# Decoder step: main-stream turns half as long, attention streams reordered, two r tiles moved from plain units to a Strassen pair

## The chip, the cores and the metric

The kernel runs on one core of one Trainium2 chip. The metric is device time in microseconds for one launch; a smaller number is better. The time given is the median of several runs; the profile is of one further execution.

## The reference

One step of a one-layer hybrid decoder, all in float32. Prompt: 512 rows; samples: 8 x 4 = 32 rows; width 2048. The kernel keeps both in one activation of 544 columns.

```python
z = rmsnorm(x, g_pre) @ w_in            # 15 parts: q,k,v, index q/k/w, gates, bu,bv, cq, ra,rb,rc
# A: index scores pick k keys per query, then softmax attention over them (8 heads, 4 kv heads)
I  = einsum(relu(qi . ki), wi);  idx = top_k(I, 128 prompt / 256 sample of 2052)
oa = softmax(q k[idx]^T / sqrt(128)) v[idx]
# B: chunked mixing
ob = bu * (tril(w_s) @ rmsnorm(bv) + b_s)
# C: 4-head attention into 256 memory tokens
oc = softmax(rmsnorm(cq) mk^T / 16) mv
m  = sum over n in a,b,c of sigmoid(r_n) * ((o_n * silu(g_n)) @ w_p_n)
y  = x + m @ w_out
```

The outputs are y for prompt and samples, and the new k, v, index k, memory k and v, and the normalized bv of the samples. The prompt attends over its own 512 keys; the samples gather keys and values from a paged cache.

## The kernel before

Every large product is done in float32r with both factors split in a high and a low part, three products each (`wh x_h`, `wh x_l`, `wl x_h`). ScalarE makes the high part of a weight tile, VectorE or POOL the low part. The moving operand has 544 columns and is done in two halves of 272.

A *unit* (`columns`, L600) is one tile of 128 output columns: 16 k-tiles, three products, two halves. A *pair* (class `Pair`, L503) is two such tiles done by Strassen's scheme: seven products of half size in place of eight.

The work is staged, and each stage ends when all its streams have ended:
- memory keys and values and the transposed activations;
- the middle stage, "in": 41 units for qi, ki, cq, then k, v, q, then bv, followed by `NI` = 43 of the 48 r tiles (r tiles go through a sigmoid and out to DRAM, `r_done`, L823);
- "turn": `NT` = 3 more r units while the operands for Strassen's scheme are formed on VectorE;
- "fast": 17 pairs: bu and bg, cg, ag, and last what is left of the r tiles, 48 - 43 - 3 = 2, one pair;
- merge, and the output projection.

Each engine works through its instructions in the order in which the program issues them, and this order is made by `Flow.run` (L206) when the program is built. Main stream and side streams are Python generators. `Flow` keeps an estimated clock for every engine. In each round every side stream whose due time has been reached gets up to six steps, then the main stream gets one step, up to its next `yield`. In `columns` that is every second k-tile, so twelve products. `yield due(t)` waits until the estimate says that tile t is ready; `yield have("x")` until flag x is set; `yield idle(a)` until VectorE's estimated clock is no more than a us ahead of TensorE's.

The side streams of the middle stage, in their order:
- `post_stream`: the job of every finished z tile: rope, norms, transposes, stores (`job_k`, `job_q`, `job_bv`; flags `kvq0` to `kvq3`, `bv`);
- `att_stream` (L1742): the index scores of samples and prompt, four memory heads (`mem_attend`, L1591), the mixing of branch B (which waits for `bv`), four prompt heads (`attend`, L1527);
- `prompt_choice`: the prompt's top-k on VectorE, throttled by `idle`;
- `sample_stream`: `sample_choice` (32 rounds of max, index, replace on VectorE), `sample_work`: gather keys, dot products on VectorE, softmax, gather values on POOL's queue, products `ps<-v` on TensorE;
- `cross_stream`: the samples' attention into the memory cache, mostly dot products on VectorE, throttled.

PSUM for side work: two banks `pa`, one `pp`, one `ps`. `post_stream` uses `pp`, the attention `pa`, the sample and cross streams `ps`. A softmax row block is `softmax_rows`: scale and maximum on VectorE, exponential on ScalarE, reciprocal and product on VectorE.

Of the kernel before, what the change touches and what calls it, by code (L numbers as in the profile page):

```python
# [34 lines left out]
NW3 = 2  # L35
NZ = 3
PI = 0.5
NI, NT = 43, 3
NG = 5
NX, CA, CD, MA, MB = 3, 4, 6, 4, 0  # L40
SLACK = 0.4
# [193 lines left out]
def decoder_step(  # L235
# [364 lines left out]
    def columns(w, c0, m, kts, rhs, done, cond=None, ready=None, over=None):  # L600

        n = PW // 128
        parts = [(w[h * n * 128:(h + 1) * n * 128, c0:c0 + m].rearrange("(k p) c -> p k c", p=128), n, m)
                 for h in range(kts // n)]

        def emit(z, h, hl):
            for kk in range(n):
                kt = h * n + kk
                if ready and not ready(kt)():
                    yield ready(kt)  # L610
                xh, xl = rhs(kt)
                if ready:
                    yield due(xl)
                for wt, xt in ((0, 0), (0, 1), (1, 0)):
                    for a in range(2):
                        PE.matmul(z[:m, a, :TH], hl[wt][:, kk, :], (xh, xl)[xt][:, a * TH:(a + 1) * TH],
                                  start=(kt == 0 and wt + xt == 0), stop=(kt == kts - 1 and wt == 1))
                if over:
                    over()
                if kk % 2 == 1:  # L620
                    yield

        return Unit(parts, emit, lambda z: done(z[:, :, :TH]), cond)

# [440 lines left out]
    def rope_rows(src, blk, cos, sin, p):  # L1065

        sw = TP_("sw")
        for b in range(p // blk):
            o, i = b * blk, (b ^ 1) * blk
            S.copy(sw[o:o + blk], src[i:i + blk])  # L1070
        V.tensor_mul(src[:p], src[:p], cos[:p])
        G.tensor_mul(sw[:p], sw[:p], sin[:p])
        yield due(sw)
        V.tensor_add(src[:p], src[:p], sw[:p])

# [66 lines left out]
    def norm_rope(zc, tb):  # L1142

        tp = yield from prompt_tr(zc)
        y = v4(TP_("y"))
        S.copy(y, tp)
        ss = sm([128, 4], "ss4", bufs=2)
        for t in range(4):
            S.activation(junk_a, y[:, t, :], AF.Square, accum_out=ss[:, t:t + 1])
        yield due(ss)  # L1150
        r = rsqrt(ss, 128, 128, 4)
        for t in range(4):
            V.tensor_scalar(y[:, t, :], y[:, t, :], r[:, t:t + 1], None, op0=OP.mult)
        o, u = v4(TP_("yo")), v4(TP_("yu"))
        V.tensor_mul(o[:, :, :64], y[:, :, :64], tb[:, 0])
        V.tensor_mul(u[:, :, :64], y[:, :, 64:], tb[:, 1])
        G.tensor_mul(u[:, :, 64:], y[:, :, :64], tb[:, 3])
        V.tensor_mul(o[:, :, 64:], y[:, :, 64:], tb[:, 2])
        V.tensor_sub(o[:, :, :64], o[:, :, :64], u[:, :, :64])
        yield due(u)  # L1160
        V.tensor_add(o[:, :, 64:], o[:, :, 64:], u[:, :, 64:])
        yield due(o)
        return o
# [361 lines left out]
        V.tensor_scalar(p_ap, p_ap, ri, None, op0=OP.mult)  # L1525

    def attend(g):  # L1527
        yield have("kvq%d" % g, "sel1", "sel2", "sel3")
        raws = []
        for d, c in ((k_d, g), (q_d, 2 * g), (q_d, 2 * g + 1), (v_d, g)):  # L1530
            raw = v4(PT("araw"))
            SP.dma_start(raw, rows4(d)[:, :, c * 128:(c + 1) * 128])
            raws.append(raw)
        parts = []
        for raw in raws:
            yield due(raw)
            if raw is not raws[3]:
                tp = yield from psum("pa")
                for t in range(4):
                    tr(tp[:, t * 128:(t + 1) * 128], raw[:, t, :])  # L1540
                yield due(tp)
                raw = v4(tp)
            hl = KK(), KK()
            split_from(v4(hl[0]), v4(hl[1]), raw)
            parts.append(hl)
        kk, qq, vv = parts[0], parts[1:3], parts[3]
        yield due(vv[1])
        for blk in range(4):
            nk = (blk + 1) * 128
            cols = slice(blk * 128, (blk + 1) * 128)  # L1550
            ss = []
            for r in range(2):
                s = yield from psum("pa")
                mm3(s[:, :nk], [x[:, cols] for x in qq[r]], [x[:, :nk] for x in kk])
                ss.append(s)
            pts = []
            for r in range(2):
                yield due(ss[r])
                pt = PT()
                mx = sm([128, 1], "mx")  # L1560
                V.tensor_tensor_reduce(pt[:, :nk], ss[r][:, :nk], selb[blk], 1.0, TAKEN, OP.add, OP.max, mx)
                softmax_rows(pt[:, :nk], mx, SA)
                pts.append(pt)
            yield due(*pts)
            pT = {}
            for k0 in range(0, blk + 1, 2):
                n = min(2, blk + 1 - k0)
                tp = yield from psum("pa")
                for kb in range(n):
                    for r in range(2):  # L1570
                        tr(tp[:, kb * 256 + r * 128:kb * 256 + (r + 1) * 128],
                           pts[r][:, (k0 + kb) * 128:(k0 + kb + 1) * 128])
                yield due(tp)
                ph, pl = PH(), PH()
                split_from(ph[:, :n * 256], pl[:, :n * 256], tp[:, :n * 256])
                for kb in range(n):
                    pT[k0 + kb] = [x[:, kb * 256:(kb + 1) * 256] for x in (ph, pl)]
            yield due(pl)
            o = yield from psum("pa")
            for kb in range(blk + 1):  # L1580
                mm3(o[:, :256], [x[:, kb * 128:(kb + 1) * 128] for x in vv], pT[kb],
                    start=kb == 0, stop=kb == blk)
            yield due(o)
            ot = OT()
            S.copy(ot, o[:, :256])
            yield due(ot)
            SP.dma_start(oa_d.rearrange("(h d) t -> d h t", d=128)[:, 2 * g:2 * g + 2, cols],
                         ot.rearrange("p (r q) -> p r q", r=2))
        flags["att%d" % g] = 1

    def mem_attend(h):  # L1591
# [27 lines left out]
        mk = KK(), KK()  # L1619
        split_from(mk[0], mk[1], tp)  # L1620
        yield due(mk[1], cq[1][1])
        for b2 in range(2):
            s = yield from psum("pa")
            for bb in range(2):
                blk = b2 * 2 + bb
                for dt in range(2):
                    mm3(s[:, bb * 256:(bb + 1) * 256], [x[:, blk * 128:(blk + 1) * 128] for x in cq[dt]],
                        [x[:, dt * 256:(dt + 1) * 256] for x in mk], start=dt == 0, stop=dt == 1)
            yield due(s)
            pt = PT()  # L1630
            S.copy(pt, s)
            mx = sm([128, 2], "mx2", bufs=2)
            V.tensor_reduce(mx, pt.rearrange("p (b m) -> p b m", b=2), axis=AX.X, op=OP.max)
            for bb in range(2):
                softmax_rows(pt[:, bb * 256:(bb + 1) * 256], mx[:, bb:bb + 1],
                             cms[:, h, b2 * 2 + bb:b2 * 2 + bb + 1])
            yield due(pt)
            tp = yield from psum("pa")
            for mt in range(2):
                for bb in range(2):  # L1640
                    tr(tp[:, mt * 256 + bb * 128:mt * 256 + (bb + 1) * 128],
                       pt[:, bb * 256 + mt * 128:bb * 256 + (mt + 1) * 128])
            yield due(tp)
            ph, pl = PH(), PH()
            split_from(ph, pl, tp)
            yield due(pl)
            o = yield from psum("pa")
            for dt in range(2):
                for mt in range(2):
                    mm3(o[:, dt * 256:(dt + 1) * 256],  # L1650
                        [x[:, mt * 256 + dt * 128:mt * 256 + (dt + 1) * 128] for x in mv],
                        [x[:, mt * 256:(mt + 1) * 256] for x in (ph, pl)], start=mt == 0, stop=mt == 1)
            yield due(o)
            ots = OT(), OT()
            for dt in range(2):
                S.copy(ots[dt], o[:, dt * 256:(dt + 1) * 256])
            yield due(*ots)
            for dt in range(2):
                SP.dma_start(oc_d[(2 * h + dt) * 128:(2 * h + dt + 1) * 128, b2 * 256:(b2 + 1) * 256], ots[dt])
# [82 lines left out]
    def att_stream():  # L1742
        yield from sample_index()
        yield from prompt_index()
        for h in range(4):
            yield from mem_attend(h)
        yield from mixing()
# [660 lines left out]
```

## Time and profile before

| | |
|---|---|
| median of 3 runs | 2300.39 us (2296.32 to 2301.41) |
| the profiled execution, time | 2297.85 us |
| its span, first to last instruction | 2296.1 us |
| granted TensorE clock, mean | 0.992 |
| PE / PEld busy | 2223.4 / 2138.6 us |
| DVE / ACT / POOL busy | 1686.7 / 964.5 / 283.8 us |

PE is TensorE's products, PEld its weight loads, DVE VectorE, ACT ScalarE, POOL GpSimd, SP the queue that issues most DMAs. Products are pipelined, so the mean duration of one (some 290 ns) is longer than the distance from one to the next, and a busy PE is not a PE at its peak. Names such as `z<-x,whi` are the tiles written and read: `z` the accumulator of a unit, `zs` that of a pair, `pa`, `pp` and `ps` the side banks. The whole kernel issues through one helper, so all rows have line L61; tiles tell the operations apart.

### The profile page before, as it was taken

To read this page: it belongs to the slowest core of one execution; us is meant where nothing else is said; L and a number is where in the kernel's file an instruction comes from. 1 tells how busy PE (TensorE), PEld (TensorE's weight loads), DVE (VectorE), ACT (ScalarE), POOL (GpSimd) and SP (SyncE) were. 2 spreads that over 40 slices of the span, in tenths; PEclk is the share of its full clock that TensorE was granted. 3 is DMA by queue.
4 is the path that set the end of the run, shared out by engine and by line. 5 is a ranking of instruction groups with operands and counts; after the bars stand their busy time and mean duration, and the time that the engine had idled before them with its cause. 6 is when DMAs were issued, how large, how long until landed. Compare 5 with 4: busy or idle time off the path is not lost. (4 is left out here: it accounts for less than half of the span.)

```text
span 2296.1 us, 46130 instructions
## 1 busy us (share of the span) xinstructions
PE 2223.4 (97%) x17057; PEld 2138.6 (93%) x17057; DVE 1686.7 (73%) x4658; ACT 964.5 (42%) x1944; POOL 283.8 (12%) x275
## 2 busy tenths in 40 slices
PE   8899999899999999999999998999999999999999
PEld 6699999899999998999999985999999999999999
DVE  7843557999889899666889514998899635567786
ACT  6544454454454432444544322444444422233443
POOL 1121220010010011001333343000000001200000
PEclk9999999999999999999999999999999999999999
DMA  7654434556556766446788776344454645444453
GB/s 245 220 173 109 124 101 112 167 147 190 164 170 197 221 196 189 137 122 180 251 272 272 221 214 173 100 127 134 128 163 143 204 135 172 143 132 136 128 158 88
DMA packets 497535, 382.17 MB, mean 166 GB/s; under 512 B 35786, under 2 KB 427068, under 8 KB 497308
## 3 DMA queue, kind: packets, MB, share of 16 engines
q1 hardware_dynamic: 485532, 341.45, 50.7%
q0 software_dynamic: 11776, 37.76, 5.0%
q8 instruction: 134, 2.20, 0.4%
q14 instruction: 93, 0.76, 0.1%
HBM read 329.81 MB, written 49.30 MB: 165 GB/s over the span
## 5 line engine op out<-in xcount | busy, mean ns | idle before, releaser
L61 PE MATMUL z<-x,whi 128*128 128x272 f32 (+1 forms) x5696 | 960.9, 291 | 0.0
L61 PEld LDWEIGHTS z<-x,whi 128*128 128x128 f32 (+1 forms) x5696 | 805.9, 188 | 19.3 <-issue 12.6
L61 DVE TENSOR_TENSOR wlo<-raw,whi 128x512 fp32r<-128x512 f32 (+1 forms) x613 | 427.0, 706 | 274.7 <-ACT whi L61 264.8
L61 ACT CAST whi<-raw 128x512 fp32r<-128x512 f32 (+1 forms) x660 | 402.8, 619 | 537.8 <-PE z L61 349.3
L61 PE MATMUL z<-x,wlo 128*128 128x272 f32 (+1 forms) x2848 | 589.8, 289 | 0.9 <-DVE wlo L61 0.9
L61 PEld LDWEIGHTS z<-x,wlo 128*128 128x128 f32 (+1 forms) x2848 | 445.5, 189 | 1.3 <-DVE wlo L61 1.3
L61 PE MATMUL zs<-x,whi 128*128 128x272 f32 x1536 | 293.5, 289 | 2.2 <-ACT whi L61 1.4
L61 PEld LDWEIGHTS zs<-x,whi 128*128 128x128 f32 x1536 | 242.6, 189 | 2.7 <-ACT whi L61 1.7
L61 PE MATMUL zs<-x,wlo 128*128 128x272 f32 x768 | 223.0, 290 | 1.3 <-DVE wlo L61 1.3
L61 ACT CAST whi<-wsum 128x512 fp32r<-128x512 f32 x192 | 119.2, 622 | 131.7 <-PE zs L61 97.3
L61 PE MATMUL zs<-oh,wlo 128*128 128x272 f32 x576 | 167.0, 290 | 1.7 <-DVE wlo L61 1.7
L61 PE MATMUL zs<-oh,whi 128*128 128x272 f32 x576 | 167.0, 290 | 0.2 <-ACT oh L61 0.2
L61 PE MATMUL zs<-ol,whi 128*128 128x272 f32 x576 | 165.6, 288 | 0.4 <-DVE ol L61 0.4
L61 PE MATMUL z<-oh,whi 128*128 128x272 f32 x768 | 159.2, 289 | 3.7 <-DVE zc L61 2.6
L61 PE MATMUL z<-ol,whi 128*128 128x272 f32 x768 | 158.8, 288 | 0.4 <-DVE ol L61 0.2
L61 PE MATMUL z<-oh,wlo 128*128 128x272 f32 x768 | 158.4, 287 | 0.0
L61 PEld LDWEIGHTS zs<-x,wlo 128*128 128x128 f32 x768 | 145.0, 189 | 1.5 <-DVE wlo L61 1.5
L61 DVE TENSOR_TENSOR wlo<-wsum,whi 128x512 fp32r<-128x512 f32 x181 | 121.5, 683 | 13.8 <-ACT whi L61 13.8
L61 POOL TENSOR_TENSOR wlo<-raw,whi 128x512 fp32r<-128x512 f32 x47 | 63.5, 1352 | 526.8 <-ACT whi L61 431.3
L61 PEld LDWEIGHTS z<-oh,whi 128*128 128x128 f32 x768 | 120.4, 188 | 4.1 <-issue 2.8
L61 PEld LDWEIGHTS z<-ol,whi 128*128 128x128 f32 x768 | 120.7, 189 | 0.8 <-DVE ol L61 0.8
L61 PEld LDWEIGHTS z<-oh,wlo 128*128 128x128 f32 x768 | 120.2, 188 | 0.0
(340 smaller groups left out, 3119.7 us busy)
## 6 DMA issues: line engine op xcount, KB each, us to landing
raw<-in_w_in_dram SPq DMA_DIRECT2D x480, 256.0 KB, 3.2
raw<-in_w_mem_kv_dram SPq DMA_DIRECT2D x64, 256.0 KB, 4.9
qbc<-cqs_d SPq DMA_DIRECT2D x64, 256.0 KB, 5.0
qbc<-qs_d SPq DMA_DIRECT2D x32, 512.0 KB, 5.6
raw<-in_w_out_dram SPq DMA_DIRECT2D x64, 256.0 KB, 2.7
kc<-in_cache_mem_k_dram SPq DMA_DIRECT2D x32, 256.0 KB, 4.5
raw<-in_w_pb_dram SPq DMA_DIRECT2D x32, 256.0 KB, 2.6
raw<-in_w_pc_dram SPq DMA_DIRECT2D x32, 256.0 KB, 2.7
```

The lines of the kernel that those rows point to most:

```text
L61: r = f(*args, **kwargs)
```

## The change

The constant `NI` goes from 43 to 41, so two r tiles more are left for pairs: the fast stage has 18 pairs. The main stream yields after every k-tile. Two kinds of multiplication go from POOL to VectorE. `att_stream` waits for all k, v, q and bv tiles before the memory heads. In `attend` the scores of a block are issued ahead of the transposes of the block before; transposes and outputs go to bank `pp`. In `mem_attend` both score groups are issued first, then both softmaxes, then transposes and outputs, the outputs in `pp`.

```diff
-NI, NT = 43, 3
+NI, NT = 41, 3
@@ columns
-                if kk % 2 == 1:
-                    yield
+                yield
@@ rope_rows
-        G.tensor_mul(sw[:p], sw[:p], sin[:p])
+        V.tensor_mul(sw[:p], sw[:p], sin[:p])
@@ norm_rope
-        G.tensor_mul(u[:, :, 64:], y[:, :, :64], tb[:, 3])
+        V.tensor_mul(u[:, :, 64:], y[:, :, :64], tb[:, 3])
@@ attend
-        yield have("kvq%d" % g, "sel1", "sel2", "sel3")
+        yield have("kvq%d" % g, "sel1", "sel2", "sel3", "bv")
...
-        for blk in range(4):
+
+        def scores(blk):
             nk = (blk + 1) * 128
-            cols = slice(blk * 128, (blk + 1) * 128)
             ss = []
             for r in range(2):
                 s = yield from psum("pa")
-                mm3(s[:, :nk], [x[:, cols] for x in qq[r]], [x[:, :nk] for x in kk])
+                mm3(s[:, :nk], [x[:, blk * 128:nk] for x in qq[r]], [x[:, :nk] for x in kk])
                 ss.append(s)
+            return ss
+
+        ss = yield from scores(0)
+        for blk in range(4):
...
                 pts.append(pt)
+            if blk < 3:
+                ss = yield from scores(blk + 1)
             yield due(*pts)
...
-                tp = yield from psum("pa")
+                tp = yield from psum("pp")
...
-            o = yield from psum("pa")
+            o = yield from psum("pp")
@@ mem_attend
+        ss = []
         for b2 in range(2):
             s = yield from psum("pa")
...
-            yield due(s)
+            ss.append(s)
+        pts = []
+        for b2 in range(2):
+            yield due(ss[b2])
             pt = PT()
-            S.copy(pt, s)
+            S.copy(pt, ss[b2])
...
+            pts.append(pt)
+        for b2, pt in enumerate(pts):
             yield due(pt)
             tp = yield from psum("pa")
...
-            o = yield from psum("pa")
+            o = yield from psum("pp")
@@ att_stream
         yield from prompt_index()
+        yield have("kvq3", "bv")
         for h in range(4):
             yield from mem_attend(h)
```

## Rows read from the trace of the kernel before

**Rows 1.** The page, part 1: busy us (share of the span) x instructions.
```profile
PE 2223.4 (97%) x17057; PEld 2138.6 (93%) x17057; DVE 1686.7 (73%) x4658; ACT 964.5 (42%) x1944; POOL 283.8 (12%) x275
```
**Rows 2.** Busy time by stage: PE, PEld, DVE, ACT, POOL, PEclk, DMA share, GB/s.
```profile
141.00:1378.00 1237.00, 1204.85 (x9466) 1166.96 (x9464) 916.31 (x3285) 537.58 (x1174) 213.85 (x211) 0.99 0.61 178
1378.00:1410.00 32.00, 25.33 (x105) 4.81 (x104) 1.88 (x13) 3.47 (x6) 19.60 (x21) 0.95 0.68 199
...
1462.00:1811.00 349.00, 348.52 (x2759) 348.52 (x2760) 316.40 (x528) 163.52 (x276) 14.56 (x11) 1.00 0.49 142
```
**Rows 3.** The chain that ended last: start us, us, what.
```profile
1403.41 3.61 DMA v<-in_cache_v_dram,gidx
...
1462.48 348.64 PE zs L61 x2758
```
**Rows 4.** Timeline of TensorE, end of the middle stage: start us, us, instruction.
```profile
1309.35 1.06 PE L61 MATMUL ps<-v,qbc 128*32 128x512 f32 x8
...
1372.64 1.07 PE L61 MATMUL ps<-v,qbc 128*32 128x512 f32 x8
...
1378.34 1.07 PE L61 MATMUL ps<-v,qbc 128*32 128x512 f32 x8
...
1410.25 0.75 PE L61 MATMUL z<-x,whi 128*128 128x272 f32 x4
```
**Rows 5.** Timeline of POOL in the same stretch, two gathers of cached values.
```profile
1398.41 0.95 POOL L61 DMA_INDIRECT v<-in_cache_v_dram,gidx  x1 [0.30 <-issue]
1399.66 0.94 POOL L61 DMA_INDIRECT v<-in_cache_v_dram,gidx  x1 [0.30 <-DMA v<-in_cache_v_dram,gidx]
```
**Rows 6.** Busy time in three stretches of the middle stage, columns as above.
```profile
400.00:926.00 526.00, 499.05 (x3884) 482.19 (x3883) 480.73 (x1462) 220.28 (x568) 42.40 (x45) 0.99 0.63 183
926.00:1080.00 154.00, 153.70 (x1210) 151.19 (x1209) 95.86 (x311) 76.26 (x130) 6.93 (x8) 0.99 0.47 134
1080.00:1281.00 201.00, 199.83 (x1592) 198.93 (x1591) 174.21 (x1183) 86.65 (x150) 68.27 (x64) 1.00 0.86 274
```
**Rows 7.** Tiles of the side streams: count, ns min/median/max, first and last start us.
```profile
L61 DVE MAX8 hold<-hold x32: 1211/1224/1227, 366.9 to 925.4; 64x8 f32<-64x1028 f32 x32
...
L61 DVE SCALAR_TENSOR_TENSOR junk_v<-kgat,qbc x512: 277/286/324, 1080.0 to 1280.6; 128x128 bf16<-128x128 f32 x171
...
L61 SPq DMA_DIRECT2D mraw<-mk_d x4: 418/438/506, 521.5 to 701.2; - x4
...
L61 SPq DMA_DIRECT2D vr<-bv_d x8: 384/430/1532, 766.4 to 888.5; - x8
...
L61 SPq DMA_DIRECT2D araw<-k_d x4: 422/442/461, 920.8 to 1166.6; - x4
```
**Rows 8.** Waits of TensorE, 360 to 950 us: us in total, times, longest.
```profile
PE pa L61 <- DVE ph L61: 5.4, 2, 5.3
```
**Rows 9.** Busy time 520 to 760 us of tiles pt, kk, ph: PE, PEld, DVE, ACT.
```profile
520.00:760.00 240.00, 5.52 (x32) 3.63 (x32) 11.05 (x24) 15.71 (x40) 0.99 0.62 179
...
520.00:760.00 240.00, 28.29 (x192) 25.24 (x192) 10.88 (x16) 9.86 (x16) 0.99 0.62 179
...
520.00:760.00 240.00, 15.17 (x96) 13.29 (x96) 5.45 (x8) 4.58 (x8) 0.99 0.62 179
```
**Rows 10.** The tile yu of the k and q norms, columns as in rows 7.
```profile
L61 DVE TENSOR_TENSOR yo<-yo,yu x24: 409/412/421, 424.4 to 662.2; 128x256 f32<-128x256 f32 x24
L61 POOL TENSOR_TENSOR yu<-y,rtab x12: 872/901/927, 423.0 to 654.9; 128x256 f32<-128x256 f32 x12
L61 DVE TENSOR_TENSOR yu<-y,rtab x12: 946/962/967, 423.2 to 655.1; 128x256 f32<-128x256 f32 x12
```
**Rows 11.** Timeline of ScalarE: a table load and the sigmoid of an r tile.
```profile
1060.78 1.28 ACT L61 ACT_TABLE_LOAD   x1
1062.08 0.62 ACT L61 ACTIVATE rz<-z 128x544 f32<-128x544 f32 x1
```

More of the change, by code (lines that the diff above doesn't have):

```diff
@@ L1553, in attend @@
                 s = yield from psum("pa")
-                mm3(s[:, :nk], [x[:, cols] for x in qq[r]], [x[:, :nk] for x in kk])
+                mm3(s[:, :nk], [x[:, blk * 128:nk] for x in qq[r]], [x[:, :nk] for x in kk])
                 ss.append(s)
+            return ss
+        ss = yield from scores(0)
+        for blk in range(4):
+            nk = (blk + 1) * 128
+            cols = slice(blk * 128, nk)
             pts = []
```

## The prediction

> **What bounds the kernel now.** I read the busy shares first, then the busy times by stage, then the chain that ended last, then the tensor engine's order at the end of the long middle stage. TensorE is busy for 97% of the span, VectorE for 73% [rows 1]. So time is won by less TensorE work, or where TensorE is only nominally busy. Stage by stage, the middle stage (units of `w_in` beside the attention streams) is full up to 1378 us; in the 32 us behind it TensorE runs only 105 instructions where a full stretch of that length would hold some 255, and POOL is busy for 19.6 us; from 1462 to 1811 us, the Strassen pairs, TensorE is at 100% [rows 2]. The chain that ended last begins exactly there, with a gather of cached values at 1403 us, and then is TensorE alone [rows 3].
>
> The order on TensorE says why. Until 1372.64 us the side stream's products `ps<-v` come between `z` products, eight steps in 63.3 us, 7.9 us each. After 1378.34 us there is no `z` any more: the main stream has run out of its 43 r tiles, and six more steps run alone until the next `z` at 1410.25 [rows 4]. They go at the pace of the gathers: 1.25 us from one to the next [rows 5], four to a step, so 5.0 us a step, with some 2 us of transposes at the end. So the middle stage ends when the sample stream ends, 32 us after the main stream has run dry.
>
> What holds the sample stream back is VectorE's queue: 480.7 of 526 us between 400 and 926 us (91%), 62% in the 154 us behind, 87% in the dot products up to 1281 [rows 6]. The starts of the blocks on VectorE and SP's queue [rows 7] give the order: choice of the sample's keys 367 to 925, dots 1080 to 1281, then the value stage. The attention stream runs beside it: memory heads from 521.5 (four, ready for the mixing at 766.4), mixing to 920.8, prompt heads at 920.8 to 1166.6, so 82 us each, the last ending near 1249.
>
> **The change part by part.**
>
> *One more pair.* 2758 products of the pairs took 348.64 us [rows 3], 126.4 ns each. A plain unit is 16 x 3 x 2 = 96 products, 12.1 us; two leave the middle stage: 24.3 us. A pair is 7 x 8 x 3 = 168 products: 21.2 us more in a stage where TensorE has no idle time. If the main stream set both ends, that would be only -3.1 us. But it doesn't: the main stream runs dry 24.3 us sooner, while the sample stream would still need its time.
>
> *Attention held back until the last bv unit.* The memory heads no longer run beside the k, v and q units. Their TensorE work leaves the time before the last bv: 192 products of 256 columns and 48 transposes by the counts in the code; taken at no more than a 272-column product each, 240 x 0.126 = 30 us. So does what TensorE waited there for their `ph`, 5.4 us [rows 8]. So bv is ready some 36 us sooner, near 730. Their VectorE work, 11.1 + 10.9 + 5.5 = 27.4 us for `pt`, `kk` and `ph` [rows 9], leaves the stretch in which VectorE is at 91%; after bv they take the place of mixing, at a like load. What comes back before the choice ends is 36 us at that load (27.4 in 245, 0.11): 4 us. So the choice, and the cross stream that the next step waits for, end about (27.4 - 4)/0.91 = 25 us sooner. Bounds: 0 (the attention stream fills the room at once, since the throttled streams yield to it) and 60 us (mixing's share leaves that stretch as well). I take 25, the end that the work counted in rows is nearest to.
>
> *Finer turns.* The main stream now lets the others in every 6 products (0.76 us) instead of every 12 (1.52 us). A step that has come due waits half a turn on average, so 0.38 us less each. The sample stream has some 40 such waits between 926 and 1080 and some 30 in its index part; not all are rounded up. I take 10 us for the first, 8 us for the second (it starts the choice sooner); bounds 0 and 25 for both. The loss side: side products stand nearer to the operations they wait for, and TensorE takes its queue in order, so a late VectorE stops it. The trace shows no such pair of settings; the waits that there are bound it: 5.4 us for `ph` [rows 8] gone at best, twice that added at worst. I take -5.4, and nothing for the later stages (merge has no free side work to gain from; bounds -3 and +4).
>
> *Multiplications from POOL to VectorE.* The twelve `yu` halves on VectorE take 962 ns beside POOL's 901 ns, while the like `yo` operation takes 412 [rows 10]: the two hold each other up. Alone they are two at 412, 824 ns, so VectorE loses nothing (-1.7 us over twelve). The nine in the rope of the indexer's tiles come before the choice can start, at 367 us [rows 7], and VectorE is not the limit there; I cost them at nothing, and at most 9 x 0.412 x 544/256 = 8 us on S if that room were gone.
>
> *Scores ahead, and `pp` for transposes and outputs.* This shortens a head, not TensorE's work. For the prompt heads: some 45 waits x 0.38 = 17 us, three blocks whose scores no longer wait behind the last output (about 2 us each, a turn and the six products), less 4 us because two transposed groups now share one bank: 82 becomes about 64 us. For a memory head (61 us: 245/4) half of its second block's waiting goes and the turns give 8 us: about 47. Mixing 154 becomes about 145. Sum 188 + 145 + 256 = 589 us from 730: about 1319. Bounds: the old pace, 245 + 154 + 331 = 730 us, to 1460; and 500 us if all waits rounded up vanish.
>
> The memory heads' exponentials now alternate with the r tiles' sigmoids. A table load took 1.28 us, and the sigmoid behind one began 0.02 us after it [rows 11]. With two more on the path of each head, that is 10 us: 1329. The Trainium skill (ScalarE: Activation LUTs, "What ACT_TABLE_LOAD costs") speaks against this move: it puts a switch of tables at about 2.66 us, load and drain, and advises grouping by table. By it the stream would end some 11 us later still, an estimate from that page; the trace shows the load, and no drain behind it.
>
> *The sum.* Main stream sooner by M = 24.3 + 5.4 = 30 us: dry at 1348. Sample stream sooner by S = 25 + 10 + 8 = 43 us. Each microsecond of S beyond M turns a step of 5.0 us alone into 7.9 us beside `z`, so the stage ends sooner by M + 0.63 (S - M) = 30 + 8 = 38 us, near 1372, with a tail of some 24 us left. The attention stream at 1329 is inside. -38 + 21.2 = -17 us. The profiled execution took 2297.85 us (span 2296.1 and 1.75 around it), which gives 2281; the median of the runs is 2.5 us higher, and 2300.4 - 17 = 2283. I say 2282, with 2271 to 2291 as the range of this case (S from 30 to 62).
>
> **The rivals.** *The sample stream comes no sooner (S = 0).* For it: its throttle lets the attention stream go first, and all VectorE work remains. Against: VectorE stands 38% free from 926 to 1080 [rows 6], into which work moves. Then 30 - 0.63 x 30 = 11 us are won and 21.2 paid: +10, 2310, slower. It decides below S = 16, where the gain (30 - 0.63 x 14 = 21) equals the pair.
>
> *The attention stream becomes the last to end.* It starts some 210 us later than now (730 for 521.5) and has to make that up by shorter heads. If it needs more than 659 us after bv, it ends after 1389 and the stage's gain is less than the pair's cost: slower. At a pace between (690 us) it ends at 1420: +10 + 21 = +31, 2329; at the old pace near 2370. For it: each head is a chain through four engines, and VectorE stays full. Against: those chains are made of waits that both other edits shorten. The page on tables raises its chance by a point at most.
>
> *No tail at all.* If VectorE packs well, S reaches 70 or more, and the value stage ends with the main stream at about 1352: -58 + 21 = -37, 2263. For it: 62% and 87% [rows 6] leave some 85 us of VectorE's time free between 926 and 1281. Against: the sample stream's own round trips through DRAM lie in that time.
>
> *The edits cancel.* S from about 9 to 23 gives a difference within 5 us.
>
> **How the numbers follow.** Forecast 0.50, no tail 0.17, sample stream no sooner 0.13, attention last 0.12, cancelled 0.08. A measurement of this kernel tells about 0.2% (4.6 us) from no change. Faster: the first two, less the forecast's upper edge, 0.64; same 0.10; slower 0.26. The range 2260 to 2314 leaves out half of "no tail" and "attention last", together about 0.2.
>
> **What would show it.** After: 46 r tiles become 44 on ScalarE; the main stream's last `z` of the middle stage near 1348; mraw loads start near 730; the last prompt head before 1350; the choice's last round before 905; the dots end near 1240; a tail without `z` shorter than 32 us; 18 pairs instead of 17 with TensorE still at 100%. Wrong if the tail without `z` grows, if the chain leads through `oa_d` of a prompt head instead of the value gathers, or if TensorE's waits on VectorE in the middle stage grow by more than 10 us.

## The result, and the profile after

The changed kernel takes 2285.21 us (median of 8 runs, 2280.38 to 2291.63); the kernel before took 2297.61 us beside it (8 runs, 2295.27 to 2301.41). The ratio is 0.9944, 95% interval 0.9929 to 0.9960: 12 us faster, where 2282 us (17 us faster) was forecast. The profiled execution took 2287.16 us, its span 2285.5.

The page's busy shares hardly move: TensorE has 24 instructions fewer than in [rows 1], as two units less and one pair more make 2 x 96 - 168 = 24.

```profile
PE 2217.0 (97%) x17033; PEld 2138.1 (94%) x17033; DVE 1697.1 (74%) x4684; ACT 964.6 (42%) x1945; POOL 279.0 (12%) x270
```

The chain that ended last (start us, us, what) no longer contains a gather of cached values, as it does in [rows 3].

```profile
1365.14 4.71 PE z L61 x36
1373.95 24.20 PE z L61 x194
1433.48 353.88 PE zs L61 x2811
1787.62 5.65 DMA ol<-gb_d
1804.06 195.51 PE z L61 x1557
```

TensorE's order at the end of the middle stage (start us, us, instruction) answers to [rows 4]. Every step `ps<-v` now has `z` products behind it, and 2 steps take 16.6 us. After the last side product, at 1373.35, the `z` products of the stage's last unit run on to 1376.1. There is no tail.

```profile
1353.20 1.07 PE L61 MATMUL ps<-v,qbc 128*32 128x512 f32 x8
...
1369.78 1.07 PE L61 MATMUL ps<-v,qbc 128*32 128x512 f32 x8
...
1373.35 0.60 PE L61 MATMUL ps<-ident,oc 128*128 128x128 f32 x4
1373.70 0.75 PE L61 MATMUL z<-x,whi 128*128 128x272 f32 x4
...
1413.06 0.52 PE L61 MATMUL zs<-x,whi 128*128 128x272 f32 x2 [0.76 <-ACT rz L61]
```

The tiles of the side streams, columns as in [rows 7]: the choice of keys ends at 865 (925), the dots at 1214 (1281), and the attention streams start and go as the last three lines show.

```profile
L61 ACT ACTIVATE rz<-z x44: 610/625/629, 737.3 to 1412.4; 128x544 f32<-128x544 f32 x44
...
L61 DVE MAX8 hold<-hold x32: 1214/1224/1227, 356.9 to 865.0; 64x8 f32<-64x1028 f32 x32
...
L61 DVE SCALAR_TENSOR_TENSOR junk_v<-kgat,qbc x512: 270/287/342, 990.5 to 1213.6; 128x128 bf16<-128x128 f32 x171
...
L61 SPq DMA_DIRECT2D mraw<-mk_d x4: 367/458/491, 731.2 to 865.0; - x4
...
L61 SPq DMA_DIRECT2D vr<-bv_d x8: 384/446/1633, 905.2 to 988.2; - x8
...
L61 SPq DMA_DIRECT2D araw<-k_d x4: 421/422/424, 1023.6 to 1270.8; - x4
```

**The budget.** The first product of a pair starts at 1413.06 instead of 1447.35, 34.3 us sooner; the middle stage's end moves by as much (1410.25 to 1376.1). From that first product to the first `z` of the merge, 391.0 us instead of 367.9 (1447.35 to 1815.25): 23.1 us given back. The rest is equal (481 us in both). -34.3 + 23.1 = -11.2; the spans differ by 10.6. The rows of before, with two short stops at the start of the pairs and one at their end:

```profile
1447.35 0.52 PE L61 MATMUL zs<-x,whi 128*128 128x272 f32 x2 [0.76 <-ACT rz L61]
...
1460.68 0.52 PE L61 MATMUL zs<-x,whi 128*128 128x272 f32 x2 [1.44 <-ACT whi L61]
1462.48 0.59 PE L61 MATMUL zs<-x,wlo 128*128 128x272 f32 x1 [1.28 <-DVE wlo L61]
...
1815.25 0.49 PE L61 MATMUL z<-oh,whi 128*128 128x272 f32 x2 [2.64 <-DVE zc L61]
```

What gives back 2 us more than the 21.2 of the pair is a longer stop at the start of the pairs. Busy time in short stretches of the kernel after (columns as in [rows 2]): TensorE stands for 5.46 us until the row of the wait ends, and then is granted half its clock, for 6.8 us by the clock record of the trace; the product behind the wait takes 0.60 us, twice its 0.29. That is 5.5 us and 3.4 lost at half clock, against 2.7 and 1.7 (3.4 us at half clock) in the kernel before: 4.4 us more. The wait at the end of the pairs is 0.75 us now instead of 2.64, 1.9 less. 21.2 + 4.4 - 1.9 = 23.7, where 23.1 was measured.

```profile
1420.00:1424.00 4.00, 0.00 (x0) 0.00 (x0) 3.33 (x6) 0.63 (x1) 0.00 (x0) 0.96 0.00 0
1424.00:1428.00 4.00, 3.77 (x15) 3.46 (x16) 3.21 (x5) 0.66 (x2) 0.00 (x0) 0.50 0.00 0
1428.00:1432.00 4.00, 4.00 (x25) 4.00 (x25) 3.29 (x6) 3.73 (x8) 0.00 (x0) 0.69 0.00 0
```

```profile
1424.07 0.60 PE L61 MATMUL zs<-oh,whi 128*128 128x272 f32 x1 [5.46 <-ACT oh L61]
```

### The profile page after: what moved, and what is told of

It reads as the page before. It is cut to its first block, busy times and chain, and to the rows that moved or that the text cites. A ratio compares the mean times of both kernels' runs of the same rounds, so it can differ in the third digit from the quotient of the medians.

```text
span 2285.5 us, 46118 instructions
## 1 busy us (share of the span) xinstructions
PE 2217.0 (97%) x17033; PEld 2138.1 (94%) x17033; DVE 1697.1 (74%) x4684; ACT 964.6 (42%) x1945; POOL 279.0 (12%) x270
## 4 chain that ended last, share of the span: by engine, by line
PE 74%; DVE 17%; DMA 5%; issue 3%; ACT 1%; SPq 1%; DVEq 0%; ACTq 0%
PE z L61 45%; PE zs L61 21%; DVE junk_v L61 4%; PE pa L61 4%; DVE wlo L61 3%; PE ps L61 2%; PE pp L61 2%; DVE hold L61 2%; DVE selb L61 1%; DVE sidx L61 1%; SPq L61 1%; DVE rsqt L61 1%; DMA araw<-k_d 1%; DMA raw<-in_w_in_dram 1%; DVE m L61 1%
## 5 line engine op out<-in xcount | busy, mean ns | idle before, releaser
L61 PE MATMUL z<-x,whi 128*128 128x272 f32 (+1 forms) x5568 | 944.2, 292 | 0.0
L61 PEld LDWEIGHTS z<-x,whi 128*128 128x128 f32 (+1 forms) x5568 | 789.9, 189 | 22.6 <-issue 17.3
L61 DVE TENSOR_TENSOR wlo<-raw,whi 128x512 fp32r<-128x512 f32 (+1 forms) x595 | 405.5, 693 | 243.2 <-ACT whi L61 234.0
L61 PE MATMUL z<-x,wlo 128*128 128x272 f32 (+1 forms) x2784 | 578.3, 289 | 6.3 <-DVE wlo L61 6.3
L61 PEld LDWEIGHTS z<-x,wlo 128*128 128x128 f32 (+1 forms) x2784 | 436.5, 189 | 7.8 <-DVE wlo L61 7.8
L61 PE MATMUL zs<-x,whi 128*128 128x272 f32 x1600 | 304.3, 288 | 0.8 <-ACT rz L61 0.8
L61 PEld LDWEIGHTS zs<-x,whi 128*128 128x128 f32 x1600 | 251.7, 188 | 1.1 <-ACT rz L61 1.0
L61 PE MATMUL zs<-x,wlo 128*128 128x272 f32 x800 | 231.6, 290 | 0.5 <-DVE wlo L61 0.5
L61 POOL TENSOR_TENSOR wlo<-raw,whi 128x512 fp32r<-128x512 f32 x63 | 87.9, 1395 | 840.0 <-ACT whi L61 701.9
L61 PE MATMUL zs<-oh,whi 128*128 128x272 f32 x600 | 175.4, 292 | 5.5 <-ACT oh L61 5.5
```

Source lines behind the costliest of these rows:

```text
L61: r = f(*args, **kwargs)
```

## The experiments

The runs were made in three sets, each beside its own runs of the kernel before: `NI` alone, the changed kernel without the pair, and coarse turns (median of before 2299.4 us); no wait, old attention, POOL, and fine turns in the middle stage (2307.0); the rest (2307.1). So ratios are compared, and places in traces of different sets only roughly: the changed kernel itself ends its middle stage at 1376 us in its first trace and at 1383 in that of the third set, and TensorE is idle 32.3 and 37.9 us between 129 and 1340 us.

### What is the tail worth? NI alone, in the kernel before

```diff
-NI, NT = 43, 3
+NI, NT = 41, 3
```

> The kernel before with NI = 41 in place of 43 and nothing else: one pair more, two plain units less in the middle stage. Theory (the sample stream's value stage ends the middle stage): the main stream runs dry 24 us sooner, the value stage gains 9 us from running alone for longer, the pair costs 21 us: about +12 us, 2310, with a tail without z of some 47 us. Rival (the main stream sets both ends, so a pair is simply cheaper than two units): -3 us, 2295.

Measured 1.0030 (1.0019 to 1.0042), 7 us slower. The main stream runs dry at 1349.7 and the next `z` starts at 1399.43: a tail of 50 us. The stage ends 10.8 us sooner than at 1410.25, and the prediction's pricing says 24.3 x 0.37 = 9.0 us for M = 24.3, S = 0. So the price of a step, alone or beside `z`, holds to 2 us.

```diff
-NI, NT = 43, 3
+NI, NT = 45, 3
```

> The kernel before with NI = 45: one pair less, two plain units more in the middle stage. Theory: the two units fill the 32 us in which TensorE has almost nothing to do; the value stage goes on beside z at 7.9 us a step and ends near 1425, the stage ends some 15 us later and 21 us of pair are saved: -6 us, 2291, with no tail. Rival (main stream sets both ends): +3 us, 2300.

Measured 0.9951 (0.9937 to 0.9965): 11 us faster, as much as the whole change. The gap without `z` shrinks to 13 us (1408.3 to 1421.35); the stage ends 11 us later and a pair is saved. The kernel before simply had two r tiles too few beside its slow sample stream.

### The changed kernel without the pair

```diff
-NI, NT = 41, 3
+NI, NT = 43, 3
```

> The changed kernel with NI = 43: the other edits without the pair. In the changed kernel the main stream and the value stage end together, so theory: +24 us in the middle stage, -21 us for the pair, +3 us against the changed kernel, 2288. Rival (the edits alone are the whole gain and the pair costs, as it would with a sample stream that still ends last): -10 us or more against the changed kernel, 2275.

Measured 0.9962 (0.9949 to 0.9975); its interval overlaps with that of the change. By the medians the pair is worth 4 us, by the prediction 24.3 - 21.2 = 3. From the first pair's product to the merge this kernel, with its 17 pairs, takes 371.8 us (1430.92 to 1802.70), 3.9 more than the kernel before: that is the stop, and with it in both kernels the pair costs 391.0 - 371.8 = 19.2, its 21.2 less the 1.9 by which it shortens the wait at the stage's end (2.64 us without it).

### Coarse turns again, and fine turns in the middle stage alone

```diff
-                yield
+                if kk % 2 == 1:
+                    yield
```

> The changed kernel with a yield after every second k-tile again (turns of 12 products). Theory (a side step waits half a turn): the sample stream's value stage ends some 18 us later and the prompt heads get longer by 10 to 15 us each; a tail of 15 us or more comes back: about +13 us against the changed kernel, 2298. Rival (finer turns only bring side products nearer to what they wait for): TensorE's waits in the middle stage shrink and the time is the changed kernel's or a few us less, 2280 to 2285.

Measured 0.9981 (0.9972 to 0.9990): fine turns are worth some 8 us of the 12. Without them the sample stream still isn't last (its last side product at 1367.9, the main stream's end near 1383): what they bring here is TensorE's time. It is idle 39.8 us in 129 to 1340 us, as against 28.5 in the kernel without the pair, of the same set and with fine turns. The sample stream itself is no later at the end of its dots:

```profile
L61 DVE MAX8 hold<-hold x32: 1212/1224/1226, 365.5 to 869.5; 64x8 f32<-64x1028 f32 x32
...
L61 DVE SCALAR_TENSOR_TENSOR junk_v<-kgat,qbc x512: 269/289/411, 1001.9 to 1209.3; 128x128 bf16<-128x128 f32 x171
```

```diff
-                yield
+                if kk % 2 == 1 or "in" not in ended:
+                    yield
```

> The changed kernel with finer turns in the middle stage alone; the units of the turn stage and of the merge yield after every second k-tile, as before. In the changed kernel TensorE waits 5.5 us for an operand of the Strassen scheme (oh) in the turn stage, which it did not before. Theory (the operands start late because the weights of that stage are no longer made ready in an idle tail; the turns have no part in it): 2285, the wait stays. Rival (finer turns push casts and subtractions of weights ahead of the operands on VectorE): the wait is gone, -5 us, 2280.

Measured 0.9945 (0.9933 to 0.9957), the ratio of the change itself: the later stages neither gain nor lose, and the wait for `oh` stays at 5.5 us. It isn't made by the finer turns.

### The memory heads not held back until bv

```diff
     def att_stream():
         yield from sample_index()
         yield from prompt_index()
-        yield have("kvq3", "bv")
```

> The changed kernel without the wait for kvq3 and bv ahead of the memory heads: they start near 520 us again, beside the jobs of k, v and q. Theory (the wait moves 27 us of VectorE work out of the stretch in which the choice is made, and TensorE's waits on late splits with it): the choice ends some 25 us later, near 890, the value stage some 25 us later, a tail comes back: +12 to +16 us against the changed kernel, 2298 to 2301. Rival (the wait only delays the attention stream, the other edits are enough): the prompt heads end 100 us sooner, the sample stream is no later, and the time is the changed kernel's or less, 2280 to 2285.

Measured 0.9969 (0.9956 to 0.9981): the wait is worth 6 us, half of what was expected of it. The mechanism is there: without it the choice ends 52 us later and the dots 33 us later than in the kernel after, and the tail is back (no `z` from 1373.2 to 1392.0).

```profile
L61 DVE MAX8 hold<-hold x32: 1211/1222/1225, 362.9 to 916.5; 64x8 f32<-64x1028 f32 x32
...
L61 DVE SCALAR_TENSOR_TENSOR junk_v<-kgat,qbc x512: 274/285/294, 1048.1 to 1246.7; 128x128 bf16<-128x128 f32 x171
...
L61 SPq DMA_DIRECT2D mraw<-mk_d x4: 452/476/507, 497.7 to 662.4; - x4
...
L61 SPq DMA_DIRECT2D araw<-k_d x4: 384/527/687, 902.2 to 1144.1; - x4
```

### The attention code of before under the new wait

`attend` and `mem_attend` are the old functions whole; the diff's core:

```diff
 def attend(g):
-            if blk < 3:
-                ss = yield from scores(blk + 1)
             yield due(*pts)
...
-                tp = yield from psum("pp")
+                tp = yield from psum("pa")
 def mem_attend(h):
-            ss.append(s)
-        pts = []
-        for b2 in range(2):
-            yield due(ss[b2])
+            yield due(s)
```

> The changed kernel with attend and mem_attend as before (scores behind the last block's output, all in bank pa), wait and finer turns kept. Theory (prompt heads are long chains that need the shortening, since they start 100 us later): a memory head gets 8 us and a prompt head some 6 us longer, the last prompt head ends near 1385 instead of 1330, behind the main stream's last z; the stage ends 10 to 20 us later: 2296 to 2305. Rival (finer turns alone shorten the heads enough): the attention ends before 1370 and the time stays at 2285.

Measured 1.0005 (0.9996 to 1.0015): leaving out the new order costs 14 us, the most of any part, and brings the time back to that of the kernel before. Here the rival "the attention stream becomes the last to end" comes true. TensorE's order at the end of the stage: products of a prompt head (`pa`), with waits for `pt`, between the last `z` of the stage and the first of the next.

```profile
1378.12 0.41 PE L61 MATMUL z<-x,wlo 128*128 128x272 f32 x2
...
1387.42 0.33 PE L61 MATMUL pa<-ident,pt 128*128 128x128 f32 x1 [1.86 <-DVE pt L61]
1390.07 1.76 PE L61 MATMUL pa<-ident,pt 128*128 128x128 f32 x7 [2.33 <-DVE pt L61]
1392.38 2.93 PE L61 MATMUL pa<-ph,kk 128*128 128x256 f32 x12 [0.55 <-DVE ph L61]
1395.10 1.09 PE L61 MATMUL z<-x,whi 128*128 128x272 f32 x4
```

From 735.3 to 1395.3 the attention takes 660 us, and the prediction had put the point from which that rival makes the change worthless at 659. Its price of 2370 at "the old pace" was too high: with fine turns and behind bv the four old memory heads take 212 us instead of 245 (735.3 to 947.3), and the prompt heads 303 instead of 331.

### The multiplications back on POOL

```diff
-        V.tensor_mul(sw[:p], sw[:p], sin[:p])
+        G.tensor_mul(sw[:p], sw[:p], sin[:p])
...
-        V.tensor_mul(u[:, :, 64:], y[:, :, :64], tb[:, 3])
+        G.tensor_mul(u[:, :, 64:], y[:, :, :64], tb[:, 3])
```

> The changed kernel with both kinds of multiplication on POOL again. Theory (VectorE and POOL hold each other up, so VectorE gains nothing from the move to POOL): the yu half on VectorE takes 0.96 us again instead of 0.41, the time is the changed kernel's within 3 us, 2285. Rival (VectorE's queue is what the sample stream waits for, so work taken off it shows): 5 us or more faster, 2280; or, if POOL delays the norms, 5 us slower.

Measured 0.9922 (0.9906 to 0.9939): not slower but 5 us faster by the medians than the change, the rival's number, though the two intervals overlap. `yu` does take 0.96 us again. A pair of kernels from one set (next) makes it plain.

### The yardstick again, a unit more in the turn stage, and both

The changed kernel once more:

> The changed kernel once more, as the yardstick for the other runs of this chip: 0.994 of the kernel before, as in its first measurement, 0.993 to 0.996.

Measured 0.9946 (0.9932 to 0.9959), 2296.15 us.

```diff
-NI, NT = 41, 3
+NI, NT = 40, 4
```

> The changed kernel with NI, NT = 40, 4: one r tile is moved from the middle stage to the turn stage, no work added or taken. Theory (the turn stage grew from 52.2 to 57.4 us because its last operands, made on VectorE and ScalarE in some 55 us, no longer get a head start in an idle tail, so that TensorE waits 5.5 us for oh and then runs at half clock for some microseconds): 12 us more of products in that stage fill the wait, the row PE zs <- ACT oh of 5.5 us goes, and the time falls by 3 to 6 us (-0.13 to -0.26%), less what the shorter middle stage (main stream 12 us sooner, value stage at 1374) gives back as a tail, so -2 to -5 us. Rival (the 5 us of the turn stage are the pace of its products, and the wait is only a symptom; or the tail takes it all): no difference, or up to +5 us.

Measured 0.9917 (0.9904 to 0.9931), 2289.97 us, 6 us below the yardstick. The wait for `oh` is gone, and the stop and the half clock with it. Busy time from 1400 to 1440 us, the yardstick first:

```profile
1400.00:1440.00 40.00, 32.41 (x239) 31.23 (x237) 35.24 (x55) 16.70 (x30) 0.00 (x0) 0.91 0.24 67
```

```profile
1400.00:1440.00 40.00, 39.24 (x313) 39.02 (x312) 38.62 (x63) 20.23 (x35) 0.00 (x0) 1.00 0.41 113
```

From the first pair's product to the merge it takes 381.4 us (1425.32 to 1806.69), the yardstick 392.7 (1419.88 to 1812.62): 11 us won there, more than the 5.5 of the wait: the yardstick has one more stop there, of 1.3 us, and by its clock record 10.2 us at half clock, 5.1 lost, and this kernel has neither. Some 6 are given back as a tail (no `z` from 1370.1 to 1376.2).

The same, and both kinds of multiplication back on POOL (the two diffs above together):

> The changed kernel with the two kinds of multiplication back on POOL, and NI, NT = 40, 4. In the run with POOL alone the value stage ended some 11 us before the main stream (1363.9 against 1374), so that here the shorter middle stage finds room: -4 to -6 us by the turn stage's wait, and -0 to -5 us by POOL, together 4 to 10 us below the changed kernel, 0.990 to 0.992 of the kernel before. Rival (POOL and the wait make no difference): as the changed kernel within 2 us.

Measured 0.9872 (0.9856 to 0.9887), 2278.21 us: 29 us faster than the kernel before, the fastest kernel of the study, and 12 us below the kernel with `NI, NT = 40, 4` alone. These two differ in the 21 multiplications only. Busy time from 400 to 730 us, first with them on VectorE, then on POOL:

```profile
400.00:730.00 330.00, 312.22 (x2403) 306.04 (x2403) 315.82 (x1099) 139.09 (x374) 25.15 (x20) 0.98 0.66 185
```

```profile
400.00:730.00 330.00, 316.70 (x2458) 310.02 (x2457) 317.82 (x1092) 142.17 (x379) 38.58 (x34) 0.98 0.70 197
```

VectorE is at 96% in both. With the multiplications on POOL, TensorE gets 55 products more into the same stretch, 55 x 0.127 = 7 us. TensorE's waits there (us, times, longest) name it: the low parts of the weights come late from VectorE, 6.2 us as against 0.8.

```profile
PE z L61 <- DVE wlo L61: 6.2, 6, 2.1
```

```profile
PE z L61 <- DVE wlo L61: 0.8, 1, 0.8
```

The first r tile's sigmoid is 10.5 us sooner (730.3 for 740.8), and none of it is given back, since the sample stream comes sooner as well (last dot at 1197.7 for 1216.2): the tail without `z` is 3.5 us, after 6 with `NI, NT = 40, 4` alone.

### Finer turns alone, in the kernel before

```diff
-                if kk % 2 == 1:
-                    yield
+                yield
```

> The kernel before with turns of six products instead of twelve in every unit, nothing else. Prediction's term: 8 us sooner into the choice and 10 us in the sample stream's waits, so S = 18 and M = 0 to 5: as the sample stream sets the stage's end, 0.63 x 18 = 11 us, to -5 us for the bounds; 0.995 to 0.998 of the kernel before. Rival (without room on VectorE, with the memory heads still beside k, v and q, finer turns bring the sample stream nothing, and the new waits of TensorE cost): 0.999 to 1.002.

Measured 0.9933 (0.9919 to 0.9946): 15 us faster, as much as the whole change, by one line. Its tiles:

```profile
L61 DVE MAX8 hold<-hold x32: 1209/1224/1226, 359.8 to 930.7; 64x8 f32<-64x1028 f32 x32
...
L61 DVE SCALAR_TENSOR_TENSOR junk_v<-kgat,qbc x512: 276/286/297, 1055.4 to 1261.8; 128x128 bf16<-128x128 f32 x171
...
L61 SPq DMA_DIRECT2D mraw<-mk_d x4: 375/568/879, 495.2 to 686.5; - x4
...
L61 SPq DMA_DIRECT2D araw<-k_d x4: 385/420/606, 897.8 to 1117.5; - x4
```

The choice does not end sooner (930.7 for 925.4), but from there to the first dot it takes 124.7 us instead of 154.6. That is the place where the prediction had looked for 10 us from shorter waits for TensorE; that those waits are the 30 us is its reading and not shown. A tail is left (no `z` from 1378.5 to 1405.3).

## Why the prediction came out as it did

Its sign and nearly its size were right, and so was its starting point: the sample stream's late end left TensorE with little to do, and ending it sooner was worth more than the pair cost. Its sum was not: it had the sample stream still end the stage, near 1372 and with 24 us of tail, and the main stream ends it, at 1376 and with none. One term was 24 us too small and another 28 us too large, so that the number came near is in good part luck. Of its list of what would show it, the loads of `mraw` near 730 (731.2), 44 r tiles, the last prompt head before 1350 and the choice's last round before 905 came out; the dots ended 26 us sooner than the 1240 given, the tail is gone, and the last `z` near 1348 did not come (1376). Of its signs of being wrong none came: TensorE's waits on VectorE before the end of the main stream are 23.7 us, after 25.0.

**The sample stream, S = 43: measured 67 us** (the last dot at 1213.6 for 1280.6). The choice ends 60 us sooner where 25 + 8 were taken; 60 was the named upper bound, "mixing's share leaves that stretch as well", and that is what happened, since mixing now starts at 905 instead of 766. From the choice to the dots 125.5 us instead of 154.6, 29 where 10 were taken for the finer turns. In the kernel before finer turns alone bring 30 there; but the changed kernel with coarse turns takes only 132.4 (869.5 to 1001.9), so of its 29 us finer turns need not be more than 7. The dots themselves take 223 us instead of 201, -22, which no term foresaw. 15 of these 22 us are idle time of VectorE (41 us, 26 before), and most of its waits there are for ScalarE, longer than before for `kk` (8.0 for 2.5 us) and `whi` (13.6 for 9.8); in the variants the dots take 199 to 224 us, and why isn't settled.

**The main stream, M = 30: measured 2 us** (1376.1 for 1378.3, to be dry at 1348). This is the step that failed. The same stretch, from 129 us to the end of the main stream, before and after:

```profile
129.00:1378.30 1249.30, 1217.15 (x9562) 1179.11 (x9560) 919.33 (x3290) 541.23 (x1180) 214.16 (x211) 0.99 0.61 178
```

```profile
129.00:1376.10 1247.10, 1214.82 (x9468) 1162.13 (x9468) 914.58 (x3301) 533.88 (x1168) 227.73 (x220) 0.99 0.62 181
```

There are only 94 products fewer, not 192: the 105 of the old tail now stand in this stretch, (192 - 94) x 0.127 = 12 us. TensorE's idle time is the same, 32.2 and 32.3 us, where -5.4 was forecast. And there are 128.3 ns of busy time to a product instead of 127.3 (1214.82 / 9468, 1217.15 / 9562), 10 us. 12 + 5 + 10 = 27 of the 28 us. That the moved products would lengthen the main stream stood in the price of a step (7.9 us beside `z`), but not in M; for the same reason the rival "no tail" at 2263 was too cheap. What happened is that rival's mechanism: the stage ends with the main stream. The last 10 us are 127.2 to 127.5 ns (129 to 1340 us) in the kernel before and its three variants, and 128.0 to 128.6 in the changed kernel and all its variants. The products are not slower: by the start times in the trace, `z` products that follow each other within 150 ns are 125.2 ns apart in both kernels (7637 and 7341 distances). There are more longer distances between two `z` products, 248 instead of 189, which the profile counts as busy up to a product's modelled end of some 290 ns; they make 6 of the 10 us. What makes them isn't settled.

**TensorE's waits, -5.4: measured 0.** The wait for `ph` of [rows 8] is all but gone in the stretch (0.7 us), and the longest of before is shorter, but others have come. From 129 to 1376 us, us in total, times, longest, the first of before and then those of after:

```profile
PE pa L61 <- DVE qsp L61: 12.8, 5, 8.6
```

```profile
PE pa L61 <- DVE qsp L61: 8.9, 8, 4.5
PE z L61 <- DVE wlo L61: 6.3, 6, 2.1
...
PE pa L61 <- DVE kk L61: 4.0, 2, 2.6
PE ps L61 <- DVE junk_v L61: 3.3, 2, 3.1
```

The wait for `wlo` was 0.9 us before, and it comes from the multiplications, as the pair of kernels above shows. Those for `kk` and `junk_v` were 1.3 us and none.

**Multiplications, nothing: 5 to 12 us lost.** The operation's own price was right: `yu` takes 418 ns on VectorE without POOL beside it (412 forecast, 962 before, [rows 10]). But "VectorE loses nothing" looked at the twelve only and let the nine in the rope pass. And it left out that in that stretch VectorE, at 96%, makes the weights' low parts, so that what it is late with stops the main stream at once. Which of the two kinds does it wasn't tried.

**Scores ahead: the sum was right (1329 forecast, the last prompt head's last copy at 1329.5), its parts were not.** From the rows of `mraw`, `vr` and `araw` (first to last of the four, divided by three; mixing from the first `vr` to the first `araw`), us:

| kernel | memory head | mixing | prompt head |
|---|---|---|---|
| before | 59.9 | 154 | 82.0 |
| before, fine turns | 63.8 | 138 | 73.2 |
| after, without the wait | 54.9 | 138 | 80.6 |
| after, attention of before | 54.8 | 145 | 81.2 |
| after | 44.6 | 118 | 82.4 |
| forecast | 47 | 145 | 64 |

For a memory head the new order saves 10 us, and its place behind bv another 10. Mixing is 26 us shorter than under the old attention and meets the dots less (905 to 1024 as against 947 to 1092, with dots from 990 or 986 on); that the dots are the reason isn't shown, since in the kernel before it meets none and takes 154. For a prompt head the new order brought nothing that the rows show: 82.4 us, and 81.2 in the old order behind the wait; beside dots from 1050, in two kernels that differ in more than the order, 80.6 us with scores ahead and 73.2 without. So what the order is worth comes by the rows from the memory heads and from mixing; the two orders weren't run apart. Whether the shared bank `pp`, for which the forecast took 4 us, eats the prompt heads' gain wasn't tried either.

**The tables.** The forecast charged two table loads more for each memory head, and that is what came. ScalarE's loads (count, busy us, mean ns, idle before): in the kernel before one from 521 to 767 us, at the very end of the memory heads; in the changed kernel nine from 730 to 905 us, in four heads; with the old order behind the wait, 13 in the same stretch, in which its fourth head is not yet done.

```profile
L61 ACT ACT_TABLE_LOAD x1 | 1.3, 1283 | 0.0
```

```profile
L61 ACT ACT_TABLE_LOAD x9 | 11.5, 1283 | 4.4 <-DVE nm L61 4.3
```

```profile
L61 ACT ACT_TABLE_LOAD x13 | 16.7, 1283 | 20.1 <-DVE nm L61 20.0
```

So the wait puts the exponentials beside the sigmoids and costs loads, and the new order, in which both softmaxes of a head follow each other, saves some of them. The Trainium skill's rule to batch activations by table set (ScalarE: Activation LUTs, "Table sets: the hidden batching unit") thus speaks against the wait, as the prediction had read it, and for the new order, which it had not said. Over the whole kernel there are 36 loads instead of 42, since the prompt heads, from 1024 us on, have 26 where they had 38. Of the drain that its section "What ACT_TABLE_LOAD costs" adds to a load, the trace after shows nothing, as before:

```profile
750.26 1.28 ACT L61 ACT_TABLE_LOAD   x1 [1.12 <-DVE nm L61]
751.55 0.60 ACT L61 ACTIVATE pt<-pt,nm,cms 128x256 f32<-128x256 f32 x1
```

**The pair, +21.2: 19.2; the turn stage, 0: 4 us lost.** The operands of the pairs are made on VectorE and ScalarE from the end of the middle stage on, and the three units of the turn stage cover 37 us of that in both kernels. The last operand (`ol`) starts 47.7 us after that end in the kernel before and 52.9 us after it here; it is 47.7 to 48.6 in the kernels in which the sample stream leaves a tail of 13 us or more, and 52.9 in all where none was left and three units follow. So without a tail the operands come some 5 us later, and TensorE stops at `oh`; the prediction had no line for it. Why they come later is not shown: the tail of before holds little that is made ahead for the turn stage, one low part of a weight on VectorE (1379.66). The stop of 5.5 us stands in every kernel without a tail and with three units (after, fine turns in the middle stage alone, without the pair, coarse turns, POOL) and in none with a longer tail or four units.

**Do the parts add?** No. Against the kernel after, leaving out one part costs 8 us (turns), 6 (wait), 14 (order), 4 (pair), and leaving out the multiplications gains 5; that adds up to 27, where the change brought 12. Against the kernel before, fine turns alone bring 15 and two r tiles fewer in pairs 11, each as much as the whole. Both bear on the same 32 us of tail (27 and 13 are left), so they need not add up; the two together weren't run. That the parts left out add up to more than the whole has another reason: some of them pay for others. Without the new order the change is worth nothing, because behind the wait the old heads end last; so a good part of the order's 14 us is the price of the wait. The change without both wait and order wasn't run.

## What to carry to other kernels

When an idle tail closes, price what then ends the stage: the work of the tail moves into the main stream and lengthens it, and the operands of the next stage can lose the cover that the tail gave them. Price a move between engines by what else the receiving engine owes to the critical one in that stretch, not by the moved operation alone. And before building several edits against one stall, try the smallest alone: here one `yield`, or one constant, gave as much as all of them.

## What was not expected of the hardware

After a stop of 5.46 us TensorE was granted 0.50 of its clock (1.2 of 2.4 GHz) for 6.8 us, in the yardstick's trace for 6.8 and, behind a second stop of 1.3 us, for 3.4 more: 6.8 us of stops and 5.1 lost to the clock, where filling them won 11 between the first pair's product and the merge. The two short stops of the kernel before, 1.44 and 1.28 us, were followed by 3.4 us at half clock, and the like two in the kernel before with `NI = 41` by none. And a VectorE that is at 96% in two kernels can differ by 55 TensorE products in 330 us: the busy share doesn't show whose work is late.
